# RWKV7 on TensorE: the triangular inverse taken from 64 to all 128 tokens of a chunk, and four matmul groups moved from array tiles to the full array

## The chip, the cores and the metric

One core of a Trainium2 chip runs the whole program. The metric is the device time of one execution in microseconds; three executions of the kernel before took 2989.6, 2992.32 and 2996.26 us, so its median is 2992.32 us. A separate execution was recorded by the hardware profiler.

## The reference

Two blocks follow each other on 512 tokens of width 2048. The first has a forgetting attention layer and a sliding window attention layer. The second projects the tokens to 65 blocks of 128 columns, which feed two branches: RWKV7 (8 units of two heads of width 64) and HGRN2 (8 units). The branches are gated, joined, projected back and normalised. The change touches RWKV7 alone. Its recurrence over tokens is, for each head:

```
sa = S @ a_t
S  = S * w_t + sa b_t^T + v_t k_t^T
o_t = S @ r_t
```

The kernel computes it in 4 chunks of 128 tokens. Inside a chunk the values u_t = S a_t of all tokens depend on each other through a strictly triangular 128x128 matrix for each head, so u = (I - A)^-1 z, where z holds what the state at the chunk's start and the tokens' v contribute. With u known, the state at the chunk's end and the outputs are plain matrix products.

## The kernel before

The kernel writes its instructions in an order found while it is built. A main stream (`stream`, line 383) goes through the projection blocks, 128 columns each: 16 slices of the contraction, and for each slice three matmuls of 128x128 weights on 512 tokens (`mm3`, line 296; high and low parts of the fp32 values, `proj<-hh,wh`, `proj<-hl,wh`, `proj<-hh,wl`). I call such a triple a slot. Between two slots `side` (line 362) puts the next step of any thread whose inputs a model of the engines (`Clock`, line 30) holds to be ready. So attention, RWKV7 and HGRN2 work stands in small groups between projection slots, and on every engine the instructions run in the order in which they were issued. Weight slices are loaded by SP (`raw`), copied by ScalarE (`wh`), and their low part is made by GpSimd (`wl`), at most three slices ahead.

A RWKV7 unit (`rwkv_unit`, line 1280) is one such thread, `M` (line 1719). Its steps, with the names that its tiles have in the rows:

- `m_step` and `m_zo` (lines 1440 and 1456), for each of 4 chunks: the triangular matrices (`yh` and `kt`) and the products of `kt` with the tokens' v (`tokv`), which give z and a part of the output (`zo`). `m_zo` writes each product as two halves of 64 rows: 8 matmuls a chunk.
- `inv_out` to `inv_in3`: the 16x16 diagonal blocks go through memory to VectorE, which inverts them (`inv_8` and `inv_16`, lines 1486 and 1497, tile `invt`, one burst of 22 instructions for a unit), and come back into the tile `wd` (`S["W"]`, 64 columns for each of 8 matrices) and `td` (`S["T"]`).
- `lev16`, `lev16b`, `lev32`, `lev32b` (lines 1541 to 1590): the inverse grows from 16 to 64 tokens. Each 128x128 matrix then has two inverted diagonal blocks of 64, one for each half of the partitions.
- the recurrence, for each chunk: `ch_z` (the state's part of z, tiles `sbd` and `chz`), `ch_u` (u of the first 64 tokens, tile `chu`), `ch_u2` (their effect on the z of the other 64), `ch_u3` (u of those), `ch_s` (the new state) and `ch_o` (the output). Each of `ch_z`, `ch_u`, `ch_u2`, `ch_u3` and `ch_s` is a few matmuls and then a VectorE instruction, on which the next step waits.

An fp32 matmul stands as two instructions in a trace (two loads and two matmuls), a transpose as one. A matmul whose operands use 64 or fewer rows or columns of the array runs on a part of it; a row of the trace gives that part, as 64*64 or 128*64 (rows by columns).

Of the kernel before, what the change touches and what calls it, by code (L numbers as in the profile page):

```python
# [11 lines left out]
ALU = mybir.AluOpType  # L12
# [4 lines left out]
T = 512  # L17
# [174 lines left out]
class Timed:  # L192
    def __init__(self, clock, nc):
# [5 lines left out]
BANKS = dict(p_lora="ss", m_step="ss", lev64="s", lev_m="s", **dict.fromkeys(  # L199
    ("p_kk2", "p_bonus", "p_tok", "m_zo", "lev16", "lev16b", "lev32", "lev32b", "ch_z", "ch_u",  # L200
     "ch_u2", "ch_u3", "ch_s", "f_3", "tok", "state", "fin3"), "t"))


class Kern:
# [928 lines left out]
    def mix_setup(self):  # L1133
        nc = self.nc

        zero = []

        def zeroed(name, shape):
            t = self.P(name, shape)
            zero.append(t)  # L1140
            return t
        self.norm_tmp = lambda: (self.P("pq"), self.P("pt"))
        self.last_ev = None
        self.raw_t = zeroed("raw", (128, 513))
# [12 lines left out]
        self.y = [[None] * KT, [None] * KT]  # L1157
# [122 lines left out]
    def rwkv_unit(self, st, u):  # L1280
# [4 lines left out]
        sgt, kt, ly, mat = self.sgt, self.kt, self.ly, self.mat[u % 2]  # L1285
        c4 = lambda t: t.rearrange("p (c t) -> p c t", c=4)

# [126 lines left out]
        own = [slice(0, 64), slice(64, 128)]  # L1414
# [134 lines left out]
        def lev16b():  # L1549
            W, t32 = S["W"], S["T"][:, :, 32:64]  # L1550
            p = ps("t", (128, 8, 32))
            for b, bs in enumerate(quarter):
                first = slice(32 * b, 32 * b + 16)
                o = 32 * (b % 2)
                for j in range(8):
                    mm(p[first, j, 0:16], y16[bs, j, :], W[bs, j, o + 16:o + 32], True, True)
                    if b % 2 == 0:
                        mm(p[bs, j, 16:32], W[bs, j, 0:32], y16[bs, j, :], True, True)
            for b, bs in enumerate(quarter):
                first = slice(32 * b, 32 * b + 16)  # L1560
                o = 32 * (b % 2)
                if b % 2:
                    nc.vector.tensor_copy(W[first, :, o + 16:o + 32], p[first, :, 0:16])
                else:
                    nc.scalar.activation(W[first, :, o + 16:o + 32], p[first, :, 0:16], AF.Copy)
                    nc.vector.tensor_tensor(out=t32[bs, :, 0:16], in0=p[bs, :, 16:32],
                                            in1=t32[bs, :, 0:16], op=ALU.add)
# [10 lines left out]
        def lev32b():  # L1578
            W = S["W"]
            p = ps("t", (128, 8, 32))  # L1580
            for a, b in (quarter[0:2], quarter[2:4]):
                for j in range(8):
                    mm(p[a, j, :], y32[b, j, :], W[b, j, 32:64], True, True)
            nc.vector.tensor_copy(W[quarter[0], :, 32:64], p[quarter[0]])
            nc.scalar.activation(W[quarter[2], :, 32:64], p[quarter[2]], AF.Copy)

        lo, hi = slice(0, 64), slice(64, 128)
# [9 lines left out]
        def block_u(c, rr):  # L1599
            p = ps("t", (128, 128))  # L1600
            for h in range(2):
                hs = slice(64 * h, 64 * h + 64)
                mm(p[rr, hs], S["W"][rr, 2 * c + h, :], S["z"][rr, hs], True, True)
            nc.vector.tensor_copy(S["u", c][rr, :], p[rr, :])

        def ch_u(c):
            def f():
# [3 lines left out]
                block_u(c, lo)  # L1611
            return f

        def ch_u2(c):
            def f():
                p = ps("t", (128, 128))
                for h in range(2):
                    hs = slice(64 * h, 64 * h + 64)
                    mm(p[hi, hs], mat[lo, 2 * c + h, hi], S["u", c][lo, hs], True, True)
                z = S["z"][hi, :]  # L1620
                nc.vector.tensor_tensor(out=z, in0=p[hi, :], in1=z, op=ALU.add)
            return f

        def ch_u3(c):
            def f():
                block_u(c, hi)
# [5 lines left out]

        def ch_s(c):
            def f():
                p = ps("t", (128, 128))
                for h in range(2):
                    hs = slice(64 * h, 64 * h + 64)
# [4 lines left out]
                for h in range(2):  # L1642
                    hs = slice(64 * h, 64 * h + 64)
# [7 lines left out]
        def ch_o(c):  # L1651
            def f():
# [5 lines left out]
                for h in range(2):  # L1658
                    hs = slice(64 * h, 64 * h + 64)
# [63 lines left out]
        for c in range(4):  # L1723
# [3 lines left out]
            if c < 3:  # L1727
# [13 lines left out]
                 (lev32b, (), None))  # L1741
        for c in range(4):
            if c:
                M += seq((ch_z(c), (), None))
            M += seq((ch_u(c), (), None),
                     (ch_u2(c), (), None),
                     (ch_u3(c), (), "w" if c == 3 else None))
# [57 lines left out]
    def hgrn_unit(self, st, u):  # L1805
# [60 lines left out]
        def lev64():  # L1866
# [167 lines left out]
        if u == 0:  # L2034
# [3 lines left out]
                 (lev64, (), None),  # L2038
# [314 lines left out]
```

## Time and profile before

| | us |
|---|---|
| median of three executions | 2992.32 |
| the profiled execution | 2993.78 |
| its span, first to last instruction | 2992.0 |
| TensorE busy in it (98%) | 2926.8 |
| VectorE busy (51%) | 1518.8 |
| GpSimd busy (45%) | 1353.5 |
| ScalarE busy (42%) | 1256.3 |
| mean granted clock of TensorE | 0.988 |

PE is TensorE's matmul side, PEld its weight loads, DVE VectorE, ACT ScalarE, POOL GpSimd, SP the queue that issues the DMAs. Since one helper issues every instruction, all of them carry line 178; the tiles' names tell them apart (`out<-in,weights` for a matmul). The RWKV7 steps stand between about 1725 and 2415 us of the span.

### The profile page before, as it was taken

To read this page: it belongs to the slowest core of one execution; us is meant where nothing else is said; L and a number is where in the kernel's file an instruction comes from. 1 tells how busy PE (TensorE), PEld (TensorE's weight loads), DVE (VectorE), ACT (ScalarE), POOL (GpSimd) and SP (SyncE) were. 2 spreads that over 40 slices of the span, in tenths; PEclk is the share of its full clock that TensorE was granted. 3 is DMA by queue.
4 is the path that set the end of the run, shared out by engine and by line. 5 is a ranking of instruction groups with operands and counts; after the bars stand their busy time and mean duration, and the time that the engine had idled before them with its cause. 6 is when DMAs were issued, how large, how long until landed. Compare 5 with 4: busy or idle time off the path is not lost.

```text
span 2992.0 us, 48037 instructions
## 1 busy us (share of the span) xinstructions
PE 2926.8 (98%) x18032; PEld 2349.3 (79%) x18032; DVE 1518.8 (51%) x3417; ACT 1256.3 (42%) x2473; POOL 1353.5 (45%) x1105
## 2 busy tenths in 40 slices
PE   8999999999999999999999999999999999999996
PEld 5788888888888888888888887777777778877785
DVE  6433334343332135555541157777877576666436
ACT  5444444444443334444443354333433345545233
POOL 3444444444445544443446554333333254544585
PEclk9999999999999999999999999999999899999998
DMA  4322332223225432222234422222222222222333
GB/s 140 106 89 89 92 92 92 89 89 92 92 85 160 149 95 78 78 74 77 81 93 155 134 92 84 66 73 69 67 63 75 69 70 77 79 75 78 103 123 106
DMA packets 192089, 275.81 MB, mean 92 GB/s; under 512 B 50576, under 2 KB 65872, under 8 KB 191856
## 3 DMA queue, kind: packets, MB, share of 16 engines
q1 hardware_dynamic: 191856, 272.73, 30.1%
q8 instruction: 142, 2.33, 0.3%
q14 instruction: 91, 0.75, 0.1%
HBM read 254.51 MB, written 18.16 MB: 91 GB/s over the span
## 4 chain that ended last, share of the span: by engine, by line
PE 89%; DVE 6%; issue 2%; DMA 1%; POOL 1%; ACT 1%; SPq 0%; POOLq 0%; DVEq 0%; ACTq 0%
PE proj L178 72%; PE t L178 7%; PE s L178 6%; PE y L178 3%; DVE invt L178 1%; DVE hh L178 1%; POOL wl L178 1%; DVE gn L178 1%; DVE ly L178 1%; DMA raw<-in_w_fox_dram 0%; DVE zo L178 0%; DVE hn L178 0%; SPq L178 0%; DMA yf<-in_x_dram 0%; DVE raw L178 0%
## 5 line engine op out<-in xcount | busy, mean ns | idle before, releaser
L178 POOL TENSOR_TENSOR wl<-raw,wh 128x512 fp32r<-128x512 f32 x847 | 1123.7, 1329 | 1575.4 <-ACT wh L178 1492.9
L178 PE MATMUL proj<-hh,wh 128*128 128x512 f32 x2624 | 1069.7, 408 | 11.0 <-ACT hh L178 6.7
L178 PE MATMUL proj<-hh,wl 128*128 128x512 f32 x2624 | 1034.1, 394 | 3.9 <-POOL wl L178 3.9
L178 PE MATMUL proj<-hl,wh 128*128 128x512 f32 x2624 | 1033.7, 394 | 3.4 <-DVE hl L178 3.3
L178 ACT ACTIVATE wh<-raw 128x512 fp32r<-128x512 f32 x848 | 530.5, 627 | 827.8 <-PE proj L178 603.8
L178 PEld LDWEIGHTS proj<-hh,wh 128*128 128x128 f32 x2624 | 496.8, 189 | 121.8 <-issue 9.6
L178 PEld LDWEIGHTS proj<-hh,wl 128*128 128x128 f32 x2624 | 496.9, 189 | 115.1 <-POOL wl L178 7.9
L178 PEld LDWEIGHTS proj<-hl,wh 128*128 128x128 f32 x2624 | 497.7, 190 | 94.8 <-DVE hl L178 6.7
L178 PE MATMUL proj<-yh,wh 128*128 128x512 f32 (+1 forms) x640 | 249.5, 390 | 0.0
L178 PE MATMUL proj<-yh,wl 128*128 128x512 f32 (+1 forms) x640 | 248.0, 388 | 0.3
L178 ACT ACTIVATE t<-t,sm 128x257 f32<-128x257 f32 (+5 forms) x256 | 133.1, 521 | 257.0 <-DVE sm L178 197.0
L178 PE MATMUL proj<-yl,wh 128*128 128x512 f32 (+1 forms) x632 | 240.9, 388 | 0.0
L178 PEld LDWEIGHTS proj<-yh,wl 128*128 128x128 f32 x640 | 120.2, 188 | 26.0 <-POOL wl L178 1.6
L178 PEld LDWEIGHTS proj<-yh,wh 128*128 128x128 f32 x640 | 120.2, 188 | 24.6 <-issue 0.9
L178 DVE TENSOR_TENSOR pt<-proj,t 128x512 f32<-128x512 f32 x32 | 22.1, 691 | 229.0 <-PE proj L178 97.2
L178 PEld LDWEIGHTS proj<-yl,wh 128*128 128x128 f32 x632 | 118.7, 188 | 24.1 <-issue 0.2
L178 DVE TENSOR_TENSOR qf<-proj,rsb 128x512 f32<-128x512 f32 x48 | 33.2, 691 | 154.4 <-PE proj L178 154.2
L178 DVE TENSOR_SCALAR t<-t,sm 128x256 f32<-128x256 f32 (+3 forms) x256 | 101.5, 417 | 6.7
L178 DVE COPY pt<-t 128x384 f32<-128x384 f32 (+1 forms) x96 | 51.3, 534 | 99.8 <-PE t L178 99.8
L178 DVE RECIPROCAL sm<-sm 128x1 f32<-128x1 f32 (+1 forms) x192 | 31.4, 163 | 117.4 <-ACT t L178 115.8
L178 PE MATMUL t<-ident,t 128*128 128x128 f32 x544 | 90.4, 272 | 0.0
L178 DVE CUSTOM_DVE_ANT_0 t<-s,c 128x128 f32<-128x128 f32 (+2 forms) x128 | 49.9, 390 | 71.9 <-PE s L178 71.9
(412 smaller groups left out, 3663.8 us busy)
## 6 DMA issues: line engine op xcount, KB each, us to landing
raw<-in_w_mix_dram SPq DMA_DIRECT2D x260, 256.0 KB, 3.1
raw<-in_w_fox_dram SPq DMA_DIRECT2D x256, 256.0 KB, 3.0
raw<-in_w_swa_dram SPq DMA_DIRECT2D x144, 256.0 KB, 3.0
raw<-in_w_foxo_dram SPq DMA_DIRECT2D x64, 256.0 KB, 3.1
raw<-in_w_swao_dram SPq DMA_DIRECT2D x64, 256.0 KB, 3.1
raw<-in_w_mixo_dram SPq DMA_DIRECT2D x64, 256.0 KB, 3.1
c<-cd SPq DMA_DIRECT2D x32, 256.0 KB, 3.8
xd<-pt SPq DMA_DIRECT2D x32, 256.0 KB, 2.4
```

Source lines behind the costliest of these rows:

```text
L178: r = f(*a, **k)
```

## The change

The inverse is carried on to all 128 tokens. `W` becomes a lasting tile of 128 columns for each matrix, zero outside what the steps write. Three new steps follow `lev32b`: `lev64` transposes the upper inverted block (8 transposes), `lev64b` multiplies it with the coupling of the two halves (8 matmuls), and `lev64c` puts the product with the lower inverted block into the upper right corner of `W` (8 matmuls). Two memsets for each unit on GpSimd keep the unused parts zero. In the recurrence `ch_u2` and `ch_u3` are gone: `ch_u` is one matmul with 128x128 weights for each head, and one VectorE copy of 128 partitions. `m_zo`, `ch_s` and `ch_o` no longer split their products into halves: `m_zo` has 4 matmuls a chunk instead of 8, `ch_s` 2 instead of 4, `ch_o` 2 (besides the one of the state) instead of 4, all with 128x128 weights. `ch_s` now multiplies across both heads and reads only the two diagonal blocks of the product.

```diff
+        self.wd = zeroed("wd", (128, 8, 128))
 m_zo:
-                        for o in (0, 64):
-                            mm(p[o:o + 64, i, hs], kt[:, h, 128 * i + o:128 * i + o + 64],
-                               S["tv"][:, c, hs], True, True)
+                        mm(p[:, i, hs], kt[:, h, 128 * i:128 * i + 128], S["tv"][:, c, hs],
+                           True, True)
 inv_in3:
-            S["W"] = P("wd", (128, 8, 64))
+            S["W"] = W
+            nc.gpsimd.memset(W[lo, :, hi], 0.0)
...
-                nc.sync.dma_start(S["W"][64 * b:64 * b + 64], bass.AP(
+                nc.sync.dma_start(W[own[b], :, own[b]], bass.AP(
 lev32b:
+            nc.gpsimd.memset(S["T"][hi], 0.0)
 new:
+        def lev64():
+            p = ps("t", (128, 8, 64))
+            for j in range(8):
+                tr(p[lo, j, :], W[lo, j, lo])
+            nc.scalar.activation(S["T"][lo], p[lo], AF.Copy)
+        def lev64b():
+            p = ps("t", (128, 8, 64))
+            for j in range(8):
+                mm(p[hi, j, :], mat[:, j, hi], S["T"][:, j, :], True, True)
+            nc.scalar.activation(S["T"][hi], p[hi], AF.Copy)
+        def lev64c():
+            p = ps("t", (128, 8, 64))
+            for j in range(8):
+                mm(p[lo, j, :], S["T"][:, j, :], W[:, j, hi], True, True)
+            nc.vector.tensor_copy(W[lo, :, hi], p[lo])
 ch_u (ch_u2 and ch_u3 go):
-                block_u(c, lo)
+                    mm(p[:, own[h]], W[:, 2 * c + h, :], S["z"][:, own[h]], True, True)
+                nc.vector.tensor_copy(S["u", c], p)
 ch_s:
-                    mm(p[hs, hs], S["tk"][:, c, hs], S["tv"][:, c, hs], True, False)
-                    mm(p[hs, hs], S["tb"][:, c, hs], S["u", c][:, hs], False, True)
+                mm(p, S["tk"][:, c, :], S["tv"][:, c, :], True, False)
+                mm(p, S["tb"][:, c, :], S["u", c], False, True)
 ch_o:
-                    for r in (0, 64):
-                        mm(o[r:r + 64, hs], mat[:, 2 * c + h, 128 + r:192 + r], S["u", c][:, hs],
-                           c == 0, c == 0 or h == 1)
+                    mm(o[:, own[h]], mat[:, 2 * c + h, 128:256], S["u", c][:, own[h]],
+                       c == 0, c == 0 or h == 1)
```

On TensorE, this is how the third chunk of the first unit's recurrence stands before, from `ch_u` to the slot behind `ch_u3` (`chz,wd` are `ch_u` and `ch_u3`, `chu,yh` into `t` is `ch_u2`):

```order
L178 MATMUL t<-chz,wd 64x64 x2
L178 MATMUL proj<-hh_96,wh 128x512
L178 MATMUL proj<-hl_111,wh 128x512
L178 MATMUL proj<-hh_96,wl 128x512
L178 MATMUL t<-chu,yh_15303 64x64 x2
L178 MATMUL proj<-hh_97,wh 128x512
L178 MATMUL proj<-hl_112,wh 128x512
L178 MATMUL proj<-hh_97,wl 128x512
L178 MATMUL t<-chz,wd 64x64 x2
L178 MATMUL proj<-hh_97,wh 128x512
L178 MATMUL proj<-hl_113,wh 128x512
L178 MATMUL proj<-hh_97,wl 128x512
```

And this is the same chunk now, from `ch_u` to `ch_o` (`tokv,tokk` and `chu,tokb` are `ch_s`, the groups into `y` `ch_o`):

```order
L178 MATMUL t<-chz,wd 128x64 x2
L178 MATMUL proj<-hh_91,wh 128x512
L178 MATMUL proj<-hl_100,wh 128x512
L178 MATMUL proj<-hh_91,wl 128x512
L178 MATMUL t<-tokv,tokk 128x128
L178 MATMUL t<-chu,tokb 128x128
L178 MATMUL y<-sbd_15306,ar_15853 128x128
L178 MATMUL y<-chu,yh_15303 128x64 x2
```

Three groups on 64x64 parts with a slot behind each became one group on the full array with one slot behind it; the state and the output follow at once.

Ahead of it the first unit's three new steps stand on TensorE, two slots apart (`ident,wd` is `lev64`, `td,yh` with 64x64 `lev64b`, `wd,td` `lev64c`):

```order
L178 MATMUL t<-ident,wd 64x64 x8
L178 MATMUL proj<-hh_97,wh 128x512
L178 MATMUL proj<-hl_113,wh 128x512
L178 MATMUL proj<-hh_97,wl 128x512
L178 MATMUL proj<-hh_90,wh 128x512
L178 MATMUL proj<-hl_98,wh 128x512
L178 MATMUL proj<-hh_90,wl 128x512
L178 MATMUL t<-td,yh_15303 64x64 x8
```

Two slots lie between `lev64` and `lev64b`, where before the recurrence's first `ch_u` followed `lev32b` directly.

On VectorE, the burst that inverts the second unit's blocks stands before in the middle of the first unit's recurrence (its last eight instructions, between `ch_u2`'s sum into `chz` and `ch_u3`'s copy into `chu`):

```order
L178 TENSOR_TENSOR raw<-proj,rsb 128x512
L178 TENSOR_TENSOR chz<-t,chz 64x128
L178 TENSOR_TENSOR invt<-ly 64x256
L178 TENSOR_REDUCE x_17025<-invt 64x32
L178 TENSOR_TENSOR invt<-ly 64x256
L178 TENSOR_REDUCE x_17025<-invt 64x32
L178 TENSOR_TENSOR invt<-ly,x_17025 64x256
L178 TENSOR_REDUCE ly<-invt 64x4x8
L178 TENSOR_TENSOR invt<-ly,x_17025 64x256
L178 TENSOR_REDUCE ly<-invt 64x4x8
L178 COPY chu<-t 64x128
```

Now the same eight stand between `lev64c`'s copy into `wd` and the first `ch_u`'s copy:

```order
L178 COPY wd<-t 64x8x64
L178 TENSOR_TENSOR invt<-ly 64x256
L178 TENSOR_REDUCE x_16995<-invt 64x32
L178 TENSOR_TENSOR invt<-ly 64x256
L178 TENSOR_REDUCE x_16995<-invt 64x32
L178 TENSOR_TENSOR invt<-ly,x_16995 64x256
L178 TENSOR_REDUCE ly<-invt 64x4x8
L178 TENSOR_TENSOR invt<-ly,x_16995 64x256
L178 TENSOR_REDUCE ly<-invt 64x4x8
L178 COPY chu<-t 128x128
```

The burst moved from one link of the unit's chain to another.

## Rows read from the trace of the kernel before

**Rows 1.** Busy time, from the page: us (share of the span) xinstructions

```profile
PE 2926.8 (98%) x18032; PEld 2349.3 (79%) x18032; DVE 1518.8 (51%) x3417; ACT 1256.3 (42%) x2473; POOL 1353.5 (45%) x1105
```

**Rows 2.** The chain that ended last, from the page: shares of the span

```profile
PE 89%; DVE 6%; issue 2%; DMA 1%; POOL 1%; ACT 1%; SPq 0%; POOLq 0%; DVEq 0%; ACTq 0%
```

**Rows 3.** Windows: start:end, length, busy us by engine, PEclk, DMA share, GB/s

```profile
1725.00:2415.00 690.00, 669.13 (x5791) 516.50 (x5790) 494.74 (x1069) 276.58 (x523) 244.04 (x189) 0.96 0.26 72
...
2000.00:2010.00 10.00, 10.00 (x109) 7.70 (x102) 5.71 (x14) 3.45 (x8) 0.61 (x1) 0.50 0.10 28
...
2365.00:2379.00 14.00, 14.00 (x132) 10.62 (x128) 4.88 (x13) 3.68 (x9) 4.62 (x7) 0.51 0.13 40
```

**Rows 4.** PE groups, 1725 to 2415 us: xcount, busy, mean ns, idle before

```profile
L178 PE MATMUL t<-tokv,kt 128*64 128x64 f32 x512 | 21.8, 228 | 0.0
...
L178 PE MATMUL t<-chz,wd 64*64 64x64 f32 x192 | 21.1, 230 | 6.4 <-DVE chz L178 6.3
...
L178 PE MATMUL y<-chu,yh 128*64 128x64 f32 x256 | 14.7, 237 | 0.8 <-DVE chu L178 0.8
```

**Rows 5.** Timeline of PE: start us, duration us, engine, operation, tiles, shape, xcount

```profile
1863.96 0.40 PE L178 MATMUL proj<-hh,wl 128*128 128x512 f32 x1
1864.28 0.44 PE L178 MATMUL t<-chu,yh 64*64 64x64 f32 x4
1864.65 0.50 PE L178 MATMUL proj<-hh,wh 128*128 128x512 f32 x1
1864.99 0.40 PE L178 MATMUL proj<-hl,wh 128*128 128x512 f32 x1
1865.23 0.39 PE L178 MATMUL proj<-hh,wl 128*128 128x512 f32 x1
1865.55 0.69 PE L178 MATMUL t<-tokv,kt 128*64 128x64 f32 x16
1866.16 0.44 PE L178 MATMUL t<-zo,wd 64*64 64x64 f32 x4
```

**Rows 6.** Timeline of PE at two groups of the HGRN2 stage

```profile
2499.72 0.68 PE L178 MATMUL s<-kt,tokv 128*64 128x64 f32 x8
...
2507.05 0.83 PE L178 MATMUL t<-tokb,tokk 128*128 128x128 f32 x6
```

**Rows 7.** Timeline of PE: two full-array matmuls of 128 columns

```profile
86.31 0.22 PE L178 MATMUL s<-k,q 128*128 128x128 f32 x1
86.37 0.27 PE L178 MATMUL s<-kl,q 128*128 128x128 f32 x1
```

**Rows 8.** Timeline of PEld there: their weight loads and the next

```profile
86.32 0.19 PEld L178 LDWEIGHTS s<-kl,q 128*128 128x128 f32 x1
86.42 0.19 PEld L178 LDWEIGHTS proj<-hh,wh 128*128 128x128 f32 x1
86.53 0.19 PEld L178 LDWEIGHTS proj<-hl,wh 128*128 128x128 f32 x1
```

**Rows 9.** Waits of PE, 1725 to 2415 us: us in total, times, longest us

```profile
PE t L178 <- DVE chz L178: 6.3, 5, 2.4
...
PE t L178 <- DVE chu L178: 3.3, 3, 1.6
```

**Rows 10.** Timeline of PE at the longest of them

```profile
2184.78 0.44 PE L178 MATMUL t<-chu,yh 64*64 64x64 f32 x4
...
2189.89 0.41 PE L178 MATMUL t<-chz,wd 64*64 64x64 f32 x4 [2.40 <-DVE chz L178]
```

**Rows 11.** DVE groups, 1725 to 2415 us

```profile
L178 DVE COPY chu<-t 64x128 f32<-64x128 f32 x64 | 18.3, 287 | 25.6 <-PE t L178 24.7
L178 DVE TENSOR_TENSOR invt<-ly,x 64x256 f32<-64x256 f32 x16 | 15.5, 968 | 0.6
```

**Rows 12.** POOL groups, 1700 to 2420 us

```profile
L178 POOL MEMSET kt<- 128x512 f32 x1 | 0.5, 527 | 0.0
```

**Rows 13.** ACT groups, 1725 to 2415 us

```profile
L178 ACT ACTIVATE tokk<-t 128x512 f32<-128x512 f32 x9 | 5.4, 596 | 7.0 <-PE t L178 7.0
```

More of the change, by code (lines that the diff above doesn't have):

```diff
@@ L195, in __init__ @@
             setattr(self, n, Engine(clock, getattr(nc, n), n))
-BANKS = dict(p_lora="ss", m_step="ss", lev64="s", lev_m="s", **dict.fromkeys(
-    ("p_kk2", "p_bonus", "p_tok", "m_zo", "lev16", "lev16b", "lev32", "lev32b", "ch_z", "ch_u",
-     "ch_u2", "ch_u3", "ch_s", "f_3", "tok", "state", "fin3"), "t"))
+BANKS = dict(p_lora="ss", m_step="ss", lev_64="s", lev_m="s", **dict.fromkeys(
+    ("p_kk2", "p_bonus", "p_tok", "m_zo", "lev16", "lev16b", "lev32", "lev32b", "lev64", "lev64b",
+     "lev64c", "ch_z", "ch_u", "ch_s", "f_3", "tok", "state", "fin3"), "t"))
 class Kern:
@@ L1284, in rwkv_unit @@
         S = {}
-        sgt, kt, ly, mat = self.sgt, self.kt, self.ly, self.mat[u % 2]
+        sgt, kt, ly, mat, W = self.sgt, self.kt, self.ly, self.mat[u % 2], self.wd
         c4 = lambda t: t.rearrange("p (c t) -> p c t", c=4)
+        own = lo, hi = [slice(0, 64), slice(64, 128)]
         def p_up():
@@ L1410, in p_tok @@
             return f
-        own = [slice(0, 64), slice(64, 128)]
         def m_ar():
@@ L1549, in lev16b @@
         def lev16b():
-            W, t32 = S["W"], S["T"][:, :, 32:64]
+            t32 = S["T"][:, :, 32:64]
             p = ps("t", (128, 8, 32))
             for b, bs in enumerate(quarter):
-                first = slice(32 * b, 32 * b + 16)
-                o = 32 * (b % 2)
+                first, second = slice(32 * b, 32 * b + 16), slice(32 * b + 16, 32 * b + 32)
                 for j in range(8):
-                    mm(p[first, j, 0:16], y16[bs, j, :], W[bs, j, o + 16:o + 32], True, True)
+                    mm(p[first, j, 0:16], y16[bs, j, :], W[bs, j, second], True, True)
                     if b % 2 == 0:
-                        mm(p[bs, j, 16:32], W[bs, j, 0:32], y16[bs, j, :], True, True)
+                        mm(p[bs, j, 16:32], W[bs, j, bs], y16[bs, j, :], True, True)
             for b, bs in enumerate(quarter):
-                first = slice(32 * b, 32 * b + 16)
-                o = 32 * (b % 2)
+                first, second = slice(32 * b, 32 * b + 16), slice(32 * b + 16, 32 * b + 32)
                 if b % 2:
-                    nc.vector.tensor_copy(W[first, :, o + 16:o + 32], p[first, :, 0:16])
+                    nc.vector.tensor_copy(W[first, :, second], p[first, :, 0:16])
                 else:
-                    nc.scalar.activation(W[first, :, o + 16:o + 32], p[first, :, 0:16], AF.Copy)
+                    nc.scalar.activation(W[first, :, second], p[first, :, 0:16], AF.Copy)
                     nc.vector.tensor_tensor(out=t32[bs, :, 0:16], in0=p[bs, :, 16:32],
@@ L1578, in lev32b @@
         def lev32b():
-            W = S["W"]
+            nc.gpsimd.memset(S["T"][hi], 0.0)
             p = ps("t", (128, 8, 32))
@@ L1582, in lev32b @@
                 for j in range(8):
[L1583 to L1589, printed above, removed]
+                    mm(p[a, j, :], y32[b, j, :], W[b, j, b], True, True)
+            nc.vector.tensor_copy(W[quarter[0], :, quarter[1]], p[quarter[0]])
+            nc.scalar.activation(W[quarter[2], :, quarter[3]], p[quarter[2]], AF.Copy)
+        def lev64():
[13 more added lines that the diff above has]
+            nc.vector.tensor_copy(W[lo, :, hi], p[lo])
         def ch_z(c):
@@ L1597, in ch_z @@
             return f
[L1599 to L1604, printed above, removed]
         def ch_u(c):
@@ L1610, in f @@
                 S["u", c] = P("chu", (128, 128), bufs=2)
-                block_u(c, lo)
-            return f
-        def ch_u2(c):
-            def f():
                 p = ps("t", (128, 128))
                 for h in range(2):
[L1618 to L1626, printed above, removed]
+                    mm(p[:, own[h]], W[:, 2 * c + h, :], S["z"][:, own[h]], True, True)
+                nc.vector.tensor_copy(S["u", c], p)
                 if 0 < c < 3:
@@ L1635, in f @@
                 p = ps("t", (128, 128))
-                for h in range(2):
-                    hs = slice(64 * h, 64 * h + 64)
-                    mm(p[hs, hs], S["tk"][:, c, hs], S["tv"][:, c, hs], True, False)
-                    mm(p[hs, hs], S["tb"][:, c, hs], S["u", c][:, hs], False, True)
+                mm(p, S["tk"][:, c, :], S["tv"][:, c, :], True, False)
+                mm(p, S["tb"][:, c, :], S["u", c], False, True)
                 f = S["em"][:, 1, c:c + 1]
                 new = self.sbd[(c + 1) % 2]
-                for h in range(2):
-                    hs = slice(64 * h, 64 * h + 64)
+                for hs in own:
                     if c:
@@ L1658, in f @@
                 for h in range(2):
-                    hs = slice(64 * h, 64 * h + 64)
-                    for r in (0, 64):
-                        mm(o[r:r + 64, hs], mat[:, 2 * c + h, 128 + r:192 + r], S["u", c][:, hs],
-                           c == 0, c == 0 or h == 1)
+                    mm(o[:, own[h]], mat[:, 2 * c + h, 128:256], S["u", c][:, own[h]],
+                       c == 0, c == 0 or h == 1)
             return f
@@ L1740, in rwkv_unit @@
                  (lev32, (), None),
-                 (lev32b, (), None))
+                 (lev32b, (), None),
+                 (lev64, (), None),
+                 (lev64b, (), None),
+                 (lev64c, (), None))
         for c in range(4):
@@ L1744, in rwkv_unit @@
                 M += seq((ch_z(c), (), None))
-            M += seq((ch_u(c), (), None),
-                     (ch_u2(c), (), None),
-                     (ch_u3(c), (), "w" if c == 3 else None))
+            M += seq((ch_u(c), (), "w" if c == 3 else None))
             if c < 3:
@@ L1864, in prep5, with lev_64 @@
             nc.vector.tensor_tensor(out=g[:, 2, :], in0=g[:, 0, :], in1=g[:, 1, :], op=ALU.mult)
-        def lev64():
+        def lev_64():
             p = ps("s", (128, 4, 128))
@@ L2037, in hgrn_unit @@
         E += seq((prep5, [("hq", u)] + (pre("hout", "hst") or [("mzo", 7), ("chs", 6)]), "hqk0"),
-                 (lev64, (), None),
+                 (lev_64, (), None),
                  (qk_dec, (), "hqk", 0),
```

## The prediction

> **What bounds the kernel now.** I read the busy times first, then the chain that ended last, then the RWKV7 stage alone. TensorE is busy for 98% of the span [rows 1] and is 89% of the chain [rows 2]; no other engine passes 51%. In the stage the change touches, 1725 to 2415 us, it is busy for 669 of 690 us, while DVE has 195 us free, ACT 413 and POOL 446 [rows 3]. So the stage is a queue in front of TensorE. The projection slots in it stay the same, and what the change is worth is what the small groups between them take out of TensorE's time, plus the waits of that queue, plus the clock.
>
> How much a group takes is read from the timeline, not from its busy time, since matmuls overlap. Projection matmuls start 0.23 us apart. Around one `ch_u2` of four instructions [rows 5] the starts are 1863.96, 1864.28, 1864.65, 1864.99: three steps, 1.03 us, where two would take 0.46. So this group costs 0.57 us. Its four instructions account for little of it: on one 64-column part of the array instructions stand 0.06 us apart (8 in 0.68 us with the last one's own 0.27 taken off [rows 6]), so 0.24 us for four. The other 0.33 us is leaving the full array and coming back: 0.09 on the way in, 0.13 on the way out, 0.11 on the first projection matmul. Going from one part straight to another costs less: 16 instructions of `m_zo`, 0.031 us apart (0.69 less 0.23, over 15), should take 0.50 us, and the next group starts 0.61 us after them [rows 5], so 0.12 us a change.
>
> [...]
>
> **What it removes and adds on TensorE.** First the changes of mode, counted in the two orders from the first RWKV7 matmul on. TensorE leaves the full array for a part 231 times before and 138 times now: 93 × 0.33 = 30.7 us less. It goes from one part straight to another 63 times before and 12 now: 51 × 0.12 = 6.1 us less. Together 36.8 us.
>
> Then the instructions. Going: 384 of the three `ch_u` steps (192 of them are the `chz,wd` row [rows 4]; 64 more belong to the first chunks and 128 to `ch_u2`) at 0.06 are 23.0 us. `m_zo`'s 512, `ch_o`'s 256 [rows 4] and `ch_s`'s 192 stand on two column parts in turn, 0.031 us apart: 29.8 us. Together 52.8 us. Coming, on the full array: 256 of `m_zo`, 128 of `ch_u`, 96 of `ch_s`, 128 of `ch_o`, 608 in all, fewer than the 1344 that go, but each loads 128 columns of weights. The price of one such instruction is the disputed number. With 128 moving columns six stand in 0.83 us, so 0.11 us apart [rows 6]; no row has 64 moving columns. What sets the 0.11? At 86 us two single-pass matmuls of 128 columns start 0.06 us apart [rows 7], so moving the columns isn't the limit there; but their loads and the next start at 86.32, 86.42 and 86.53 [rows 8], 0.10 to 0.11 apart whatever the matmuls need. So a full-array instruction can't go below its load, and 64 moving columns instead of 128 win nothing. I take 0.11, the bound from above; the bound from below is 0.06, the spacing when 64 columns of weights are loaded. 608 × 0.11 = 66.9 us.
>
> [...]
>
> The new steps: `lev64` has 8 transposes for each unit, 64 in all, at 0.06: 3.8 us. `lev64b` and `lev64c` have 16 instructions each for a unit, 256 in all, on one 64-column part, at the 0.06 of rows 6: 15.4 us. Their mode changes are in the 138.
>
> Sum on TensorE: 66.9 + 3.8 + 15.4 - 52.8 - 36.8 = -3.5 us. The mode changes that go pay for the wider loads and the three new steps, and little is left.
>
> **Waits.** TensorE waits in the stage 6.3 us for `chz` and 3.3 us for `chu` [rows 9]. The longest, 2.40 us, is before a `ch_u3` [rows 10], a step that goes. But where the wait comes from stays: DVE runs the burst that inverts the next unit's blocks, of instructions up to 0.97 us [rows 11], and a link of the recurrence queues behind it. In the new order the burst stands between `lev64c`'s copy and the first `ch_u`'s copy, or between two later links. Six of the eight bursts touched a unit's chain before, five do now. Each chunk has two links fewer, each unit three more for the new steps, 40 fewer in all. I take 3 us off; the bounds are 0 and the full 9.6 us.
>
> **What is beside other work.** DVE loses two instructions a chunk, 32 copies of 0.29 us [rows 11] and 32 sums like them, and gains 8 copies; it isn't the bound, so nothing by itself. ACT gains 16 copies of 64x512, about 0.6 us each by the nearest row [rows 13]; two slots, 1.4 us, stand behind each. POOL gains 16 memsets of 64x512 at 0.53 us by the nearest row [rows 12], 8.4 us, hidden by its 446 free us. Behind each on POOL stands a `wl`, for which TensorE would wait if the memset were late: by its place, TensorE has finished what the memset waits for when it is issued, so I take nothing, and at most the 8.4 us. The loads of `wd` stand at the same place in SP's queue with the same sizes; nothing.
>
> **The clock.** The stage's granted clock is 0.96 [rows 3], so about 8% of 690 us, 55 us, ran at 1.2 instead of 2.4 GHz, and half of that, 28 us, is lost. Two such stretches, 2000 to 2010 and 2365 to 2379 [rows 3], begin at `lev16b`'s many tiny matmuls, which stay, and run on through the later inverse steps. There the change puts three more small steps; in exchange 64 small steps of the recurrence go. I take zero, with 8 us to both sides.
>
> **Sum.** The profiled execution took 2993.8 us, 1.8 more than its span. 2993.8 - 3.5 - 3 = 2987.3. It was 1.5 us above the median of the runs, so the median after should be 2986 us. A measurement of this kernel tells about 0.2%, 6 us, from no change, so the border to a measurable gain is 2986.3: my forecast sits on it, with its own range of 2976 to 2996.
>
> **Rivals.**
> - Full-array instructions with 64 moving columns stand 0.06 us apart. For it: moving 64 columns needs no more, and the load could run ahead. Against: the loads of rows 8. It would take 0.05 us from 512 of the 608 instructions, 26 us: 2960 us.
> - The waits go altogether because a chunk has fewer links, and with them some time at 1.2 GHz. For it: the longest wait stood at a step that goes [rows 10]. Against: the burst is still in the chain. The other 6.6 us of waits, and 8 us of the 28 lost to the clock: 2971 us.
> - Slower: the new steps hold the clock down. `lev32`, `lev32b`, `lev64`, `lev64b`, `lev64c` now follow one another with two or three slots between them, all on parts of the array. If in five units a stretch at 1.2 GHz lasted 22 us, beyond the last new step, where the two of rows 3 last 10 and 14, that is some 50 us more at half speed, 25 us lost, and the gain of 6.5 is gone from 13 us more on. Taking two thirds of it: 2986 + 17 = 3003 us. For it: the long stretches end only after `lev32b`. Against: the 64-column steps are bigger than the 16-column ones that begin these stretches.
>
> **How the numbers follow.** Forecast 60%: of it 33 in a measurable gain, 25 within 0.2%, 2 slower. Cheap full-array instructions 8%, faster. No waits 10%, faster. Clock 22%: 18 slower, 4 within. Faster 0.51, same 0.29, slower 0.20. The range runs from 2966, below the second rival, to 3004, above the third, and leaves out the first.
>
> **What would show it.** In the new profile: `t<-chz,wd 128*128` instructions 0.11 us apart, or 0.06 for the first rival. A `ch_u` group alone between projection matmuls costing 0.45 us. `wd,td` and `td,yh` of 64 columns, 16 in about 1.2 us. Waits for `chz` and `chu` that together are some 6 us, new ones for `wd` or `td` small. The stage's granted clock between 0.95 and 0.97. The forecast is wrong if the stage's projections end over 15 us earlier or later than 6.5 us before their present place, if the mode changes cost other than 0.33 us, or if waits for POOL's `wl` grow past 5 us.

## The result and the profile after

The changed kernel took 3007.5 us (median of 4 runs, 3006.9 to 3013.1) where the kernel before took 2991.0 in the runs beside it: a ratio of 1.0051, 95% interval 1.003 to 1.0071. Forecast were 2986 us and a range of 2966 to 3004. The profiled execution took 3006.92 us, with a span of 3005.1 and a mean granted clock of 0.982 (before 0.988).

Busy time and the chain that ended last, from the page of the kernel after, answer to [rows 1, 2]:

```profile
PE 2937.5 (98%) x17616; PEld 2388.4 (79%) x17616; DVE 1494.7 (50%) x3361; ACT 1266.2 (42%) x2489; POOL 1360.7 (45%) x1122
```

```profile
PE 89%; DVE 6%; issue 2%; POOL 1%; DMA 1%; ACT 1%; SPq 0%; POOLq 0%; DVEq 0%; ACTq 0%
```

TensorE has 416 instructions fewer and is busy 10.7 us longer. Why, the windows of the kernel after show, with the columns of [rows 3]: the stage, then the stretches in it at half clock that last over 6 us:

```profile
1725.00:2415.00 690.00, 664.76 (x5201) 542.88 (x5199) 456.71 (x971) 282.78 (x528) 249.34 (x205) 0.94 0.27 72
1851.00:1859.00 8.00, 8.00 (x125) 6.62 (x120) 2.69 (x8) 1.19 (x4) 0.00 (x0) 0.57 0.01 2
2002.00:2012.00 10.00, 10.00 (x81) 7.55 (x74) 3.01 (x7) 4.63 (x10) 1.79 (x2) 0.50 0.01 2
2132.00:2138.60 6.60, 6.08 (x17) 4.95 (x18) 6.32 (x13) 0.63 (x1) 0.78 (x1) 0.51 0.00 1
2162.00:2186.00 24.00, 23.53 (x227) 18.92 (x223) 6.60 (x19) 9.46 (x19) 3.05 (x3) 0.51 0.08 23
2231.00:2238.00 7.00, 7.00 (x79) 5.87 (x79) 4.07 (x8) 1.52 (x3) 0.00 (x0) 0.53 0.05 18
2295.50:2302.00 6.50, 5.38 (x12) 3.79 (x13) 6.23 (x12) 1.98 (x4) 4.34 (x3) 0.50 0.32 87
2323.00:2330.00 7.00, 7.00 (x72) 5.47 (x72) 3.37 (x10) 2.00 (x5) 0.27 (x1) 0.52 0.01 2
```

The stage's clock is 0.94 where it was 0.96, and TensorE is busy for 664.8 of 690 us instead of 669.1: it runs slower and also stands still more. In all, some 85 us of the stage ran at half clock, before some 51. At half clock, a granted 0.50, the projections' matmuls of 512 columns start 0.427 us apart, and at a granted 1.00 0.227. Each by three steps on PE, kernel before:

```profile
2007.30 0.63 PE L178 MATMUL proj<-hh,wl 128*128 128x512 f32 x1
2007.72 0.63 PE L178 MATMUL proj<-hh,wh 128*128 128x512 f32 x1
2008.15 0.63 PE L178 MATMUL proj<-hl,wh 128*128 128x512 f32 x1
2008.58 0.63 PE L178 MATMUL proj<-hh,wl 128*128 128x512 f32 x1
```

```profile
600.17 0.39 PE L178 MATMUL proj<-hh,wh 128*128 128x512 f32 x1
600.39 0.39 PE L178 MATMUL proj<-hl,wh 128*128 128x512 f32 x1
600.62 0.39 PE L178 MATMUL proj<-hh,wl 128*128 128x512 f32 x1
600.85 0.39 PE L178 MATMUL proj<-hh,wh 128*128 128x512 f32 x1
```

Where the recorded texts have 1.2 GHz, this half clock is meant. No trace gives a clock in GHz: 512 columns in 0.427 us are 1.2 in a nanosecond, an estimate from the first four lines, and 2.4 is twice that, where the last four lines give 2.26.

The waits of PE in that stage, kernel after (us in total, times, longest), answer to [rows 9]:

```profile
PE t L178 <- DVE zo L178: 13.5, 5, 4.5
PE proj L178 <- ACT wh L178: 6.3, 2, 3.3
PE proj L178 <- POOL wl L178: 1.8, 5, 0.6
PE t L178 <- ACT zo L178: 1.4, 3, 0.5
PE t L178 <- DVE chz L178: 1.0, 1, 1.0
PE y L178 <- DVE chu L178: 0.3, 1, 0.3
```

And two lines of the same view of the kernel before, which [rows 9] leaves out:

```profile
PE proj L178 <- ACT wh L178: 3.7, 2, 3.4
...
PE t L178 <- DVE zo L178: 2.1, 3, 1.0
```

The waits for `chz` and `chu` are nearly gone. In their place PE waits for `zo`, a tile of the unit's end, which cost 2.1 us before, and somewhat longer for `wh`, the main stream's weight copies.

The PE groups of the steps that changed, 1725 to 2430 us, kernel after, answer to [rows 4]:

```profile
L178 PE MATMUL t<-tokv,kt 128*128 128x64 f32 x256 | 35.5, 285 | 0.0
L178 PE MATMUL y<-chu,yh 128*128 128x64 f32 x124 | 17.5, 264 | 0.3 <-DVE chu L178 0.3
L178 PE MATMUL t<-chz,wd 128*128 128x64 f32 x92 | 12.9, 263 | 1.5 <-DVE chz L178 1.0 <-ACT zo L178 0.5
```

What a lone `ch_u` and a lone `lev64c` cost shows the timeline of PE, kernel after, at full clock; it answers to [rows 5]:

```profile
2030.82 0.39 PE L178 MATMUL proj<-hh,wl 128*128 128x512 f32 x1
2031.05 0.55 PE L178 MATMUL t<-chz,wd 128*128 128x64 f32 x4
2031.41 0.48 PE L178 MATMUL proj<-hh,wh 128*128 128x512 f32 x1
2031.72 0.39 PE L178 MATMUL proj<-hl,wh 128*128 128x512 f32 x1
...
2188.61 0.40 PE L178 MATMUL proj<-hh,wl 128*128 128x512 f32 x1
2188.93 1.15 PE L178 MATMUL t<-wd,td 128*64 128x64 f32 x16
2190.01 0.50 PE L178 MATMUL proj<-hh,wh 128*128 128x512 f32 x1
2190.35 0.40 PE L178 MATMUL proj<-hl,wh 128*128 128x512 f32 x1
```

Three starts from 2030.82 to 2031.72 are 0.90 us, less 0.46 for two projection matmuls: the `ch_u` costs 0.44, that is 0.11 for each of its four instructions and no change of mode. `lev64c` costs 1.74 - 0.46 = 1.28 us, as the prediction's prices have it (16 instructions at 0.06 and 0.33 for the change of mode are 1.29).

**A ledger of the stage.** From each trace I took the time from projection matmul 6390 to 8700 (the same work in every kernel), half of its time at half clock (lost to the clock), the gaps between TensorE's matmuls (standing still), and what is left: TensorE's work at full clock.

| one profiled run each, us | length | lost to the clock | standing still | work at full clock |
|---|---|---|---|---|
| before | 842.5 | 25.6 | 22.5 | 794.4 |
| after | 856.6 | 42.7 | 26.9 | 787.0 |
| difference | +14.1 | +17.1 | +4.4 | -7.4 |

(Where TensorE stands still inside a stretch at half clock, 3.4 us after and 0.4 before, half of that is in both middle columns, so the last column is up to 1.7 us too low for the kernel after.) Outside the stage nothing moved by more than 2 us. So the work got shorter, as forecast, and the clock took more than twice that back.

**Where the new waits come from.** DVE at the end of the sixth unit, kernel after (the first line is the burst's last):

```profile
2292.59 0.41 DVE L178 TENSOR_REDUCE ly<-invt 64x32 f32<-64x256 f32 x1
2292.93 0.67 DVE L178 TENSOR_TENSOR zo<-y,zo 128x512 f32<-128x512 f32 x1
2293.63 0.69 DVE L178 TENSOR_REDUCE gn<-zo 128x8 f32<-128x512 f32 x1
2294.35 0.17 DVE L178 TENSOR_SCALAR gn<-gn 128x8 f32<-128x8 f32 x1
2294.56 0.69 DVE L178 TENSOR_TENSOR zo<-zo,gn 128x512 f32<-128x512 f32 x1
```

ACT behind it:

```profile
2295.28 0.63 ACT L178 ACTIVATE zo<-zo 128x512 f32<-128x512 f32 x1 [8.30 <-DVE zo L178]
2295.82 1.66 ACT L178 ACTIVATE wh<-raw 128x512 fp32r<-128x512 f32 x3
```

And PE, at the fourth unit's end and at this one:

```profile
2127.61 0.39 PE L178 MATMUL proj<-hh,wl 128*128 128x512 f32 x1
2132.52 1.09 PE L178 MATMUL t<-ident,zo 128*128 128x128 f32 x4 [4.53 <-DVE zo L178]
2133.26 0.78 PE L178 MATMUL proj<-hh,wh 128*128 128x512 f32 x1
...
2296.49 0.79 PE L178 MATMUL proj<-hh,wh 128*128 128x512 f32 x1 [3.31 <-ACT wh L178]
2297.08 0.63 PE L178 MATMUL proj<-hl,wh 128*128 128x512 f32 x1
```

The unit's end is two steps here: `f_1` (`zo` less its mean, then ACT's square of it) and `f_2` (the sums of the squares, then `zo` scaled, which TensorE's transposes of `zo` need). In four of the eight units one of them stands behind the next unit's inversion burst, or a part of it, in DVE's queue. In the sixth, above, and the seventh it is `f_1`: ACT stands 8.30 and 8.47 us at its square with the weight copies `wh` behind it, and PE stands 3.31 and 3.01 us at `wh`. In the second and the fourth `f_1` is through and it is `f_2`: PE stands 3.52 and 4.53 us at `zo`. The fifth long wait, 3.35 us for `zo` at 2227 us, has no burst in front of it: there `f_2`'s own small instructions on DVE last 1.2 us, where the same take 0.17 elsewhere, while GpSimd works. The kernel before has such a collision in three units, once with the same result (ACT 7.87 us at its square, PE 3.41 us at `wh` at 2348 us). That it costs more now because each chunk has two links fewer is argued from the order of the steps, not shown. Behind each of the five waits, 3.0 to 4.5 us, PE goes on at half clock: matmuls that last 0.39 us last 0.63.

### The profile page after: what moved, and what is told of

Read it like the earlier page. It is cut to its first block, busy times and chain, and to the rows that moved or that the text cites. A ratio compares the mean times of both kernels' runs of the same rounds, so it can differ in the third digit from the quotient of the medians.

```text
span 3005.1 us, 47200 instructions
## 1 busy us (share of the span) xinstructions
PE 2937.5 (98%) x17616; PEld 2388.4 (79%) x17616; DVE 1494.7 (50%) x3361; ACT 1266.2 (42%) x2489; POOL 1360.7 (45%) x1122
## 4 chain that ended last, share of the span: by engine, by line
PE 89%; DVE 6%; issue 2%; POOL 1%; DMA 1%; ACT 1%; SPq 0%; POOLq 0%; DVEq 0%; ACTq 0%
PE proj L178 73%; PE t L178 8%; PE s L178 6%; PE y L178 3%; DVE gn L178 1%; DVE hh L178 1%; POOL wl L178 1%; DVE invt L178 1%; DVE ez L178 0%; DVE ly L178 0%; DVE zo L178 0%; DVE hn L178 0%; DMA raw<-in_w_fox_dram 0%; POOL bk L178 0%; ACT wh L178 0%
## 5 line engine op out<-in xcount | busy, mean ns | idle before, releaser
L178 PEld LDWEIGHTS t<-ident,t 128*128 128x128 f32 x544 | 69.5, 140 | 20.5
```

The source lines that it names most:

```text
L178: r = f(*a, **k)
```

## The experiments

In the edits a tuple (1, x) behind a step makes the planner hold the thread's next step back until x us after this step's results are due. "Lost" is (1 - mean granted clock) x span of each run, its median over the runs; "rest" is the time less that. Ratios are to runs of the kernel before taken beside each. Those had medians of 2990.7 to 2993.5 us, with 32.9 to 38.9 us lost (35.9 beside e1 to e4) and a rest of 2955.5 to 2957.2.

**1. The unit's end out of the burst's way (e1, the changed kernel; e2, the kernel before).**

```diff
-            nc.scalar.activation(S["zo"][:, :, 0, :], of, AF.Square)   # in f_1
+        def f_sq():
+            nc.scalar.activation(S["zo"][:, :, 0, :], S["zo"][:, :, 1, :], AF.Square)
-(f_1, (), "rf1"), (f_2, (), None), (f_3, ...
+(f_1, (), "rf1", (1, 3.0)), (f_sq, (), None), (f_2, (), None, (1, 5.0)), (f_3, ...
```

> The changed kernel, with the end of each RWKV7 unit issued later: the Square of f_1 becomes a step of its own, 3 us later by the planner's model, and f_3's transposes stand 5 us later. TensorE's work is the same. Theory 1 (TensorE's long waits for the normalisation of the output, tile zo, and for the weight copies behind its Square cost their own time and then a stretch at 1.2 GHz each): waits for zo fall from 13.5 us to under 3, those for wh from 6.3 to under 3, time at 1.2 GHz between 1725 and 2440 us from 85 to about 60 us, together some 25 us off: about 2983 us, ratio to before 0.997. Theory 2 (the new inverse steps hold the clock down): the waits go, but the time at 1.2 GHz stays near 80 us: about 2997 us, ratio 1.002.

> The kernel before with the same later end of each unit. Its waits for zo are 2.1 us and for wh 3.7. Theory 1: little to win, 2 to 6 us: ratio 0.998 to 1.000. If the later end costs something of its own (tiles held longer), it shows here as a ratio over 1.001.

e1: 2996.3 us, ratio 1.0009 [0.9998, 1.0019], 47.9 lost. e2: 2990.1, 0.9989 [0.9979, 1.0], 44.8 lost. In e1 the waits for `zo` and most of those for `wh` went, and 11 of the 16.5 us came back. One new wait shows in its waits of PE:

```profile
PE t L178 <- ACT pq L178: 5.9, 2, 5.7
PE proj L178 <- ACT wh L178: 2.3, 1, 2.3
```

So the waits at the unit's end are part of the loss, but most of the extra clock loss stayed (12 us of 18), and the time is the one that theory 2 named.

**2. Which half of the change (e3: the changed kernel with `m_zo`, `ch_s`, `ch_o` in halves again; e4: the kernel before with these three on the full array; e7: the kernel before with `m_zo` alone so).**

```diff
e3, m_zo (ch_s and ch_o in the same way):
-                        mm(p[:, i, hs], kt[:, h, 128 * i:128 * i + 128], S["tv"][:, c, hs],
+                        for o in (0, 64):
+                            mm(p[o:o + 64, i, hs], kt[:, h, 128 * i + o:128 * i + o + 64],
e4, e7: the reverse of it
```

> The changed kernel with m_zo, ch_s and ch_o in halves again, so only the inverse to 128 tokens and the single u step are left of the change. By the sum on TensorE: m_zo wins little or nothing alone, ch_s and ch_o lose their mode changes again, so TensorE's own time is 0 to 5 us above the changed kernel's. Theory 3 (full-array instructions that wait for their loads keep the array half idle and bring the clock down): the time at 1.2 GHz falls from 85 to about 55 us, 3007 - 15 = 2992 us. Theories 1 and 2: the long waits or the new steps are still there, time at 1.2 GHz 75 us or more, about 3005 us.

> The kernel before with only m_zo, ch_s and ch_o on the full array; u in halves, no new inverse steps. The recurrence keeps its five links, so the end of a unit keeps its place. Theories 1 and 2: waits and time at 1.2 GHz as before (51 us between 1725 and 2415), ratio 0.997 to 1.001. Theory 3: time at 1.2 GHz up to 75 us or more, ratio 1.004.

> The kernel before with m_zo alone on the full array. On TensorE 256 instructions at 0.11 us come for 512 at 0.031, +12.3 us, against up to 32 round trips or changes of mode. Theory C (m_zo is the part of the full-array edits that loses, since it stood beside m_step's matmuls on parts anyway): ratio 1.003 to 1.005, the time without the clock's loss 4 to 8 us over that of before. If ch_s and ch_o lose it instead, 1.000.

e3: 2997.7, 1.0015 [1.0003, 1.0027], 50.9 lost; work in the stage 782.3. e4: 3004.8, 1.005 [1.0035, 1.0065], 43.5 lost; 800.0. e7: 3017.2, 1.0074 [1.0056, 1.0092], 54.3 lost; 802.8. Against the 794.4 of before, the longer inverse with its single u saves 12 us of TensorE's work in e3, and the wider loads cost 5 to 8 (e3 against the kernel after, e4, e7), by e7 nearly all in `m_zo`. These are single orders: other orders of one kernel differ by up to 12 us in this column (section 5), so the signs agree but the sizes are rough. Theory 3 isn't borne out: e3, with the halves back, still loses 50.9 us. And e7 has none of the new steps and loses as much to the clock as the kernel after, while e4, with the same `m_zo`, loses 43.5: neither the new steps nor the wide `m_zo` alone sets the loss.

**3. Space between the inverse's steps (e5: behind each step from `lev16` to `lev64b`; e6: also `lev16b` in two halves; e12: behind `lev32b`, `lev64` and `lev64b` alone; e9: as e6, on the kernel before).**

```diff
-(lev16, (), None), ... (lev64b, (), None)
+(lev16, (), None, (1, 2.0)), ... (lev64b, (), None, (1, 2.0))
e6 and e9 too:
-(lev16b, (), None),
+(lev16b, (), None, (0, 1.4)), (lev16c, (), None, (1, 2.0)),   # two quarters each
```

> The changed kernel with 2 us by the planner's model (some three projection slots) between each of the inverse steps lev16, lev16b, lev32, lev32b, lev64, lev64b, lev64c. Same instructions. Theory A (a stretch at 1.2 GHz begins at lev16b's tiny matmuls and lasts as long as small steps follow closely): it still begins in most units, but lasts 3.4 to 6.8 us instead of up to 24: the clock's loss over the span falls from 54 us to about 40, time about 2995 us. Theory B (the loss comes from the long waits of TensorE for zo and wh alone): the loss stays at 50 us or more unless these waits change, about 3005 us.

> As the spaced kernel, and lev16b in two halves with 1.4 us (two projection slots) between them. Eight more round trips out of the full array, 8 x 0.33 = 2.6 us. Theory A: the stretches that begin at lev16b go, only those after long waits stay: the clock's loss falls to 30 us or less, time about 2985 us. Theory B: loss 50 us or more, about 3007 us.

> The changed kernel with the 2 us of space only behind lev32b, lev64 and lev64b, so only the new steps stand apart. If the new steps hold the clock down, the loss falls from 54 us to 30 or less, about 2985 us. Theory A (lev16, lev16b and lev32 close together begin and feed the stretches, the new steps only lengthen a few): loss 40 to 52 us, about 3000 us.

> The kernel before with its inverse steps spaced and lev16b in two halves. Theory A (the density of the small inverse steps sets the clock's loss, in both kernels): the loss falls from 36 us to some 12, as in the changed kernel with the same edit; with 2 to 8 us more for groups that no longer share a mode change: 2972 to 2980 us. Against the changed kernel so edited (2965.5 us) this gives what the change itself is worth without the clock: 7 us or more in its favour by the sum on TensorE, 6.5 us, and the waits. Rival (the loss is an effect of the changed kernel alone): loss stays near 36 us, about 2992 us.

| | us | ratio [95%] | lost | work in the stage |
|---|---|---|---|---|
| e5 | 2974.7 | 0.9936 [0.9922, 0.995] | 19.3 | 798.7 |
| e6 | 2965.5 | 0.9907 [0.989, 0.9923] | 11.9 | 800.9 |
| e12 | 2975.4 | 0.9936 [0.9921, 0.9951] | 35.7 | 787.8 |
| e9 | 2982.3 | 0.9966 [0.9953, 0.9978] | 16.4 | 807.5 |

The stage's windows of e6, and then of e12:

```profile
1725.00:2415.00 690.00, 675.51 (x5505) 553.99 (x5503) 492.63 (x1055) 303.80 (x573) 261.40 (x216) 1.00 0.29 75
```

```profile
1725.00:2415.00 690.00, 678.21 (x5442) 557.10 (x5441) 486.64 (x1039) 296.43 (x560) 257.92 (x210) 0.97 0.29 73
```

And the waits for `zo` in them, e6 and then e12:

```profile
PE t L178 <- DVE zo L178: 4.9, 5, 1.1
```

```profile
PE t L178 <- DVE zo L178: 5.5, 4, 1.9
```

With no step added or taken, only held apart (and `lev16b` cut in two), the clock in the stage goes from 0.94 to 1.00, and the changed kernel becomes the fastest of all, 42 us below itself. The loss fell further than theory A had put it (to 19.3 us in e5, where about 40 was named, and to 11.9 in e6, 30 or less). e12 spaces the new steps alone: the loss goes from 54 to 36 us, the level of the kernel before and between the two forecasts, and the time is 18 us below before. That doesn't show that the new steps had held the clock down: in the kernel after only one of the eight units ran any of them at half clock (`lev64` at 2179 us), and e12's edit also took the waits for `zo` from 13.5 to 5.5 us and left none over 2 us. In exchange the work in the stage grows by 12 to 14 us in e5, e6 and e9 (and by 1 in e12), in both kernels alike. With the clock nearly out of the way in both, e6 against e9, the change is worth 17 us between the medians, in one order of each. Of that the two profiles show 13 in the stage: work 6.6 less, standing still 15.5 instead of 18.4, and 3.4 less lost.

**4. Spacing with halves kept (e8: e3 with the later end and the spacing; e10: without the later end; e11: the changed kernel with `m_zo` alone in halves, spaced).** The edits are those of 1 to 3, together.

> The inverse to 128 tokens and the single u step, with m_zo, ch_s and ch_o in halves as before, the unit's end issued later, the inverse steps spaced and lev16b in two halves. Theory A with the sum on TensorE: time without the clock's loss about 2945 us as in the version with halves, the loss under 30 us: about 2975 us, ratio 0.994, faster than both kernels. Theory B: loss 45 us, about 2990 us.

> The inverse to 128 tokens and the single u step, m_zo, ch_s and ch_o in halves as before, inverse steps spaced and lev16b in two halves; the unit's end where the planner puts it. Theory A: loss 12 to 20 us; on TensorE the version with halves took about 5 us less than the full one: about 2960 us. If a later end was what cost the earlier version of this its gain, this one is well under 2980 us; if the halves do, it stays near 2990 us.

> The changed kernel with m_zo alone in halves again, spaced and with lev16b in two halves. m_zo alone on the full array cost the kernel before 7 us without the clock's loss. Theory C: 4 to 7 us under the changed kernel so edited: about 2960 us. Rival (spaced apart, m_zo's group no longer stands next to m_step's and gains as much from the fewer mode changes as its loads cost): 2965 us, the same.

All three came out slower than expected: 2993.8 (1.0005 [0.9994, 1.0016]), 2994.6 (1.0 [0.999, 1.001]) and 2982.8 (0.9964 [0.9952, 0.9977]), with 35.9, 32.9 and 26.8 us lost. The halves saved 8 to 12 us of e6's work in the stage (791.0, 788.5 and 792.6), but TensorE stood still for 28.8, 31.7 and 24.6 us instead of 15.5, in e10 for example at these:

```profile
PE proj L178 <- ACT pq L178: 7.2, 3, 2.5
PE t L178 <- DVE zo L178: 5.9, 6, 1.3
PE t L178 <- ACT td L178: 5.8, 1, 5.8
```

Stretches at half clock of 14 to 20 us came back with them (the stage's clock is 0.97 in e8 and 0.98 in e10 and e11, 1.00 in e6). The longest wait of PE from 1725 to 2440 us is 3.4, 5.8 and 3.1 us in e8, e10 and e11, against 1.6, 1.1, 1.9 and 2.3 in e5, e6, e12 and e9. Spacing helped where the order that resulted had no such wait, and I couldn't foretell which order has.

**5. Is it the change, or the order that it happened to get? (e13, e15, e17: the changed kernel in three other orders; e14, e16, e18: the kernel before with the same shifts.)** No step is altered; one is issued a little later.

```diff
e13, e14:
-(inv_load, (), None),
+(inv_load, (), None, (1, 0.7)),
e15, e16: the same with 1.4
e17, e18:
-(f_1, (), "rf1"),
+(f_1, (), "rf1", (1, 1.4)),
```

(The number stands behind `inv_load`, so what is held back is `inv_8`; behind `f_1` it is `f_2`.)

> The changed kernel with no step altered; the second step of each unit's inversion (the load of the blocks) is only issued 0.7 us later, so the order falls differently. Theory, that the order decides by chance: the loss to the clock falls anywhere between 36 and 54 us, like those of the orders so far, and the time between 2985 and 3008. Rival, that the changed steps themselves lower the clock in any order: 50 us or more, 2998 to 3010. That the kernel after was an unlucky order: below 2995.

> The kernel before with the same 0.7 us. Theory, that the order decides by chance: a loss to the clock between 36 and 54 us, 2990 to 3010, above the 2993 of before more likely than below. Rival, that the changed steps lower the clock: the loss stays at 36 to 45, 2988 to 2998.

> The changed kernel with that load 1.4 us later. Theory (chance): 2985 to 3008, loss to the clock 36 to 54. Rival (the changed steps): loss 50 or more, 2998 to 3010.

> The kernel before with that load 1.4 us later. Theory (chance): 2990 to 3010, loss 36 to 54. Rival (the changed steps): loss 36 to 45, 2988 to 2998.

> The changed kernel with the second step of each unit's end (f_2) issued 1.4 us later and nothing else. Two other orders of it took 3013 and 3006 us, against 2986 and 2998 for the same shifts of the kernel before. Theory, that the changed steps cost in any order in which the inverse's steps stand dense: 2998 to 3013. Rival (a chance of the order): below 2995.

> The kernel before with f_2 1.4 us later. Theory (the changed steps cost): 2985 to 2999, at least 6 us below e17. Rival (chance): 3000 or more, or not below e17.

With e1, e2 and the two kernels themselves these are five dense orders of each:

| us | time | lost | standing still in the stage | work in the stage |
|---|---|---|---|---|
| before; e2; e14; e16; e18 | 2993.3; 2990.1; 2986.1; 2997.9; 2986.1 | 35.9; 44.8; 32.8; 41.9; 35.8 | 22.5; 17.6; 17.1; 20.8; 17.5 | 794.4; 790.9; 797.7; 795.2; 794.3 |
| after; e1; e13; e15; e17 | 3007.5; 2996.3; 3013.0; 3005.6; 2987.6 | 54.1; 47.9; 49.7; 60.1; 46.3 | 26.9; 22.6; 30.1; 24.6; 18.7 | 787.0; 789.3; 793.6; 781.7; 786.6 |
| mean difference, 95% | +11 (-1 to +24) | +13 (5 to 21) | +5.5 (0.1 to 11) | -7 (-12 to -1) |

(Time and lost are medians over the runs, the last two columns from one profile each.) The ratios to before are 1.0064 [1.0041, 1.0086], 1.0043 [1.0028, 1.0057] and 0.9986 [0.9971, 1.0] for e13, e15 and e17, and 0.9971 [0.9955, 0.9987], 1.0018 [1.0001, 1.0034] and 0.9982 [0.9971, 0.9994] for e14, e16 and e18. Both theories hold a part: e15, and e13 nearly, went by the one that blames the changed steps, e17 by the one that blames the order, with e18 only 1.5 us below it. The changed steps, left dense, lost more to the clock in each of their orders than the kernel before in any of its own (46.3 at least, 44.8 at most; one step of the printed clock is 3 us), and the waits for `zo` come with them in three shifts of three: 14.0, 11.0 and 8.0 us in e13, e15 and e17 against 0.9, 3.2 and 0.9 in e14, e16 and e18. e13's line, and then e14's:

```profile
PE t L178 <- DVE zo L178: 14.0, 6, 3.7
```

```profile
PE t L178 <- DVE zo L178: 0.9, 2, 0.7
```

But one order of the changed kernel is no slower than before, and the orders of one kernel differ by up to 25 us. The time's own difference isn't shown to be above zero over orders; its three terms are, the waits only just. The clock's term rests on the medians: in the ten profiles, one run each, the stage's loss differs by 4 us on the mean and not clear of noise (25.6, 37.5, 23.9, 41.0, 27.3 before, 42.7, 29.0, 32.4, 46.1, 27.3 after).

## Why the prediction was wrong

- **Sum on TensorE, -3.5 us: right within 4 us.** Over five orders 7 us less (1 to 12). `ch_u` alone costs 0.44 us where 0.45 was named, `lev64c` 1.28 where the text said about 1.2. A full-array instruction with 64 moving columns stands 0.11 us from the next, so the first rival (0.06) is refuted.
- **Waits, "I take 3 us off; the bounds are 0 and the full 9.6 us": failed.** The waits that it counted did shrink, `chz` and `chu` from 9.6 to 1.0 us. What failed is the bound of 0: the step asked which links of the recurrence queue behind the burst and left out the unit's end, which uses the same queue. There the waits grew: `zo` 13.5 us instead of 2.1, `wh` 6.3 instead of 3.7, both of them after ACT's square. Standing still rose by 4.4 us here and by 5.5 over the orders.
- **The clock, "I take zero, with 8 us to both sides": failed, and decided the sign.** 17 us more were lost in the stage, 18 in the median run. By what stood ahead of the stretches in the two profiles: those that begin around `lev16b` make up 58 us at half clock instead of 41, in seven units instead of five, and those behind TensorE's waits (five of 3.0 to 4.5 us after, three of 1.8 to 3.4 before) 27 instead of 10. Each is 17 us more at half speed, 8.5 us lost. So the waits took a second price, which the sum left out. Of the seven stretches at `lev16b` only one reaches a new step: from 2162 to 2186 it runs over `lev64`. Why more units fell at `lev16b`, which stayed as it was, is open.
- **The rivals.** The third, at 3003 us and 22%, is near in its number and had the right term, the clock. Its mechanism, five units with stretches of 22 us beyond the last new step, isn't what the profile shows: one unit has such a stretch, 24 us, and it ends as `lev64b` begins; e16, which has no new steps, has two of 24 us from `lev16b` on (41.0 us lost in its stage, clock 0.94). It also had the waits as a gain. The second (no waits, less half clock, 2971 us) comes near e6's 2965.5, but by another way: spacing, not fewer links, and TensorE still stood still for 15.5 us.
- **The trade of small steps.** The prediction let three dense new steps be paid by 64 steps that go from the recurrence. The rows don't support counting steps so: those that go stood apart, each with a slot behind it, and none of the long stretches began at them. What the steps' distance is worth is in e5, e6 and e9; no run tests the exchange by itself.
- **Its own sign of being wrong** came true: the projections end 13 us later, 19.6 from the forecast place. Two of its marks weren't met either: the stage's clock is 0.94, not 0.95 to 0.97, and the waits for `chz` and `chu` are 1.0 us, not some 6.

What makes the loss of a given order 46 or 60 us, or 33 or 45 before, isn't settled. That density raises it is shown by e5, e6 and e9, where spacing took it down in both kernels (54.1 us to 19.3 and 11.9, and 35.9 to 16.4). That long waits do is read from the half clock behind all five of 3.0 to 4.5 us in the profile of after. Which order avoids both I could only find by running it. That the changed steps themselves raise it is as strong as five orders against five, and by what path is open.

## What to carry to other kernels

Where TensorE is the bound and small matmuls stand between long ones, a change has three terms: work at full clock, standing still, and time at half clock (-7.4, +4.4 and +17.1 us in this stage). Here the first was right to 4 us and didn't matter beside the third. When a chain gets shorter, ask what its end now runs into, and space a run of small steps before judging it: in one order each the same change lost 0.5% dense and gained 0.9% spaced, of which the kernel before gets 0.3% by the same spacing. And run two or three shifted orders of both kernels before a difference below 1% is put down to the steps themselves.

## What the runs showed of the hardware

- TensorE's five waits of 3.0 to 4.5 us in the profile of after were each followed by half clock (granted 0.50 or 0.51), and so was `lev16b`, with its many tiny matmuls and no wait, in seven of the eight units there and in five before. No rule is shown: behind a wait of 2.11 us for `pq` at 2980 us in the kernel after, half clock stood within 2 us, and behind the same wait of 2.10 us at 2967 us in the kernel before the granted clock stayed at 1.00 for 5 us.
- Runs of one kernel differ by the clock: over 29 runs of the kernel before the loss has a standard deviation of 5.3 us, the rest 2.1. e6, with nothing lost in the stage and 11.9 us in all, spread by 0.9 us over four runs.
- In the burst of the kernel after, three tiny DVE instructions took as long as three of GpSimd, 1.21 us each:

```profile
2120.59 0.18 DVE L178 TENSOR_TENSOR invt<-ly 64x32 f32<-64x32 f32 x1
2120.81 1.21 DVE L178 TENSOR_TENSOR ly<-ly,invt 64x32 f32<-64x32 f32 x1
2122.05 1.21 DVE L178 TENSOR_TENSOR invt<-ly 64x30 f32<-64x30 f32 x1
2123.30 1.21 DVE L178 TENSOR_TENSOR ly<-ly,invt 64x30 f32<-64x30 f32 x1
```

GpSimd at that time, same kernel:

```profile
2120.68 3.79 POOL L178 TENSOR_TENSOR wl<-raw,wh 128x512 fp32r<-128x512 f32 x3 [3.80 <-ACT wh L178]
```

Three instructions of 1.21 us instead of 0.18 stand beside three of GpSimd that take 3.79 us together, and end with them. No run took GpSimd's work away, so that the one lengthens the other is read and not tested. The three made the burst that the unit's end waits for 3 us longer here.
